# Weight sums and token forms on VectorE, and feed-forward buffers that stay open to the end of the block

## The chip, the cores and the metric

The kernel runs on one core of one Trainium2 chip. The metric is the device time of one execution in microseconds (us); the time of a kernel is the median of its runs. The engines of the core are TensorE (PE, matrix products; PEld is its weight load), VectorE (DVE), ScalarE (ACT), GpSimd (POOL) and SyncE (SP, which issues most of the transfers). Each works through its own instruction queue in order, and they wait for each other through semaphores.

## The reference: one encoder layer

One layer is applied to 768 tokens (512 of a prompt, 256 of a sample) of width 1024, all in float32:

```
x = LN1(alpha*x + 0.5*SwiGLU1(x))          # SwiGLU: (silu(x @ Wg) * (x @ Wu)) @ Wd, inner width 2816
u = x @ W_in                                # 5888 columns: RWKV-7 group, retention group, two gates
a = RWKV7_bidir(u_a) @ W_A ; b = Retention_bidir(u_b) @ W_B
x = LN2(alpha*x + (sigmoid(g_a)*a + sigmoid(g_b)*b) @ W_out)
x = LN3(alpha*x + 0.5*SwiGLU2(x))
```

The change touches the two feed-forward blocks (FFN1 with LN1, FFN2 with LN3), what follows FFN1 (the first two column blocks of W_in), and the buffers of the merge before LN2.

## The kernel before

**Layout.** Activations lie transposed: 8 tiles `z[k]` of 128 features by 768 tokens. A float32 product is made of three products of a rounded high part and a low part (high x high, high x low, low x high). `split` (lines 186 to 188) makes the parts: ScalarE casts the high part, VectorE subtracts it. `mmt` (line 198) issues all these products.

**The up projection** (`ffn`, from line 290) works on 22 blocks of 128 inner features, index j. A block needs two weights (gate g and up u, 512 KB each, "raw" loads at line 310 into 3 buffers `wr`) and two token halves of 384 (TH). Instead of eight half products it makes seven, in Strassen's manner: "11", "21", "22", "T1", "T2", "T3", "T4". Each is 12 matmuls of 384 columns. For that, it needs sums of weights and of tokens:

- weight sums s1 to s4, one set for each block, in `combine` (line 329) on GpSimd, 128x512 each. `pieces` splits each product's weight into high and low (tiles `ph`, `pl`, 4 buffers each).
- token forms t1 to t4, once for each FFN and each of four feature pairs, in `forms` (lines 276 to 288): t1 and t3 on GpSimd, t2 and t4 on VectorE, and then split into the second half of `xs[k]` (for T1) and into `ext` (tiles `eh`, `el`: T3, T4, T2).

`head(j)` (line 332) makes product 11, `second(j, g)` (line 341) adds 21 and applies silu, `do_up(j)` (line 346) makes the rest; additions at line 360 take the products out of PSUM. The first 2 blocks of FFN1 and the first 4 of FFN2 have head and second ahead of everything (`lead`), then load their gate weight again in FFN2.

**The down projection.** The blocks go in chunks of 6, 6, 5 and 5. `do_down` adds a chunk's product into `z` for all 768 tokens; it stands behind the first block of the next chunk. `last_down` (line 392) does the last chunk by token segments (512, then 256 tokens), so that LayerNorm of one segment can run beside the product of the other. Its weights come through `wtile` (lines 157 to 159): one load, a cast, a subtraction, into a pool `wp` of 2 buffers that is opened when the up projection's pools (`fw`: raw weights, pieces, sums; `xe`: `ext`) are closed (lines 416 and 417). 4 of the 8 weights of segment 0, and the last two of the rotating ones, are reused for segment 1 (`reuse`, line 174).

**LayerNorm** (`layer_norm`, line 250): the mean over features is a product with a matrix of 1/1024 on TensorE. `token_sum` (line 236) either does this for each of 8 feature tiles (8 matmuls that accumulate, line 239), or adds the tiles on VectorE (line 246) and makes one matmul (line 248). Tables MPE (mean) and VPE (variance) choose for each LayerNorm and segment; 1 means TensorE. Then come subtraction of the mean (line 259), squares on ScalarE (line 261), the variance, an inverse root by Ln and Exp (lines 230 to 234), scaling (lines 267 and 268) and, where something follows, a split.

**What follows FFN1.** `prep` begins with two lead products of W_in, blocks 12 and 13, weights through `wp`. Their place in TensorE's queue is fixed by hand (`issue_after`): the first behind the mean of segment 1, the second behind its variance, so that they run while LayerNorm of segment 1 is made. `prep` and the retention then load all further weights through `wp`.

**The merge** before LN2 loads W_out for three segments of 256 tokens, and KEEPO of its 8 weights are kept for the later ones.

**PSUM** has 8 banks of 512 columns. In FFN1 there are two tiles of two banks ("mm", one of them in a pool `pre`) for the down products and 4 single banks ("pc") for the up products and sums. In FFN2 the same with its own pool.

**Order.** A planner orders each engine's instructions at build time, by their order in the program and by when its model holds them to be ready; inside `prep` and the FFNs nothing but the leads is pinned by hand. A pool that is opened where another was closed waits for that pool's users.

Of the kernel before, what the change touches and what calls it, by code (L numbers as in the profile page):

```python
# [17 lines left out]
P = 128  # L18
# [31 lines left out]
MPE = {1: (0, 0), 2: (0, 0, 0), 3: (0, 0)}  # L50
VPE = {1: (0, 0), 2: (0, 0, 1), 3: (0, 1)}
# [4 lines left out]
KEEPO = 2  # L56
# [9 lines left out]
class Builder:  # L66
# [169 lines left out]
    def token_sum(self, st, src, k, pe, pool):  # L236
        nc = self.nc
        if pe:
            nc.tensor.matmul(st["ps"], self.ones, src, start=k == 0, stop=k == KT - 1)
            return  # L240
# [35 lines left out]
    def forms(self, z, xs, ext, tmp):  # L276
        nc = self.nc
        for k in range(KT // 2):
            (b11, b12), (b21, b22) = ([t[:, :TH], t[:, TH:]] for t in (z[k], z[k + KT // 2]))
            ta, tb = (tmp.tile([P, T], F32, tag=t, name=self.nm("f")) for t in ("hh", "hl"))  # L280
            t1, t2, t3, t4 = ta[:, :TH], ta[:, TH:], tb[:, :TH], tb[:, TH:]
            nc.gpsimd.tensor_tensor(out=t1, in0=b12, in1=b11, op=ALU.subtract)
            nc.gpsimd.tensor_tensor(out=t3, in0=b22, in1=b12, op=ALU.subtract)
            nc.vector.tensor_tensor(out=t2, in0=b22, in1=t1, op=ALU.subtract)
            nc.vector.tensor_tensor(out=t4, in0=b21, in1=t2, op=ALU.subtract)
            self.split(t1, *(t[:, TH:] for t in xs[k]))
            self.split(tb, *(t[:, :2 * TH] for t in ext[k]))
            self.split(t2, *(t[:, 2 * TH:] for t in ext[k]))

    def ffn(self, ctx, z, xs, idx, up, down, after, lead, first, wctx, then=None):  # L290
# [5 lines left out]
        hp = self.pool(ctx, "hp", max(CHUNKS) + 3, "right")  # L296
        hs, kept, raws, open_ = {}, {}, {}, {}
# [29 lines left out]
        def combine(a, b, op):  # L327
            t = fw.tile([P, m * P], F32, tag="sa", name=self.nm("sa"), bufs=4)
            nc.gpsimd.tensor_tensor(out=t, in0=a, in1=b, op=op)  # L329
            return t  # L330

        def head(j):
            g = load(j, 0)
            s, uu = (hp.tile([P, T], F32, tag=t, name=self.nm("u")) for t in ("hh", "hl"))
            ps = self.bank()[:, :TH]
            product(ps, g[:, :m * P], "11", True)
            nc.scalar.copy(uu[:, :TH], ps)
            open_[j] = s, uu, ps
            return g

        def second(j, g):
            s, uu, ps = open_[j]
# [3 lines left out]
        def do_up(j):  # L346
# [3 lines left out]
            s, uu, _ = open_[j]  # L350
# [5 lines left out]
            pc, pd, pb = (self.bank()[:, :TH] for _ in range(3))  # L356
# [35 lines left out]
        def last_down(seg, lp, kp):  # L392
# [3 lines left out]
            fetch = lambda n, keep=None: self.wtile(down[n, :, ch[0]:ch[-1] + 1], (len(ch), P), keep)  # L396
            for i, (n, w) in enumerate(self.reuse(kept, fetch, kp, KEEP)):
# [4 lines left out]
            return mean  # L402
# [142 lines left out]
    def prep(self, fill):  # L545
# [7 lines left out]
        if True:  # L553
# [5 lines left out]
            lead = [self.mmps() for _ in range(2)]  # L559
            lw = [self.wtile(self.I["w_in"][i], (KT, P)) for i in (12, 13)]  # L560
            var = self.summed
            with self.tc.issue_after(self.mean):
                self.mm3b(lead[0], lw[0], self.xs, SEGS[:1], len(BLK[1]) > 2)
            self.tc.add_manual_dep(var, self.latest.name, mybir.DependencyInfo(
                mybir.DependencyClass.NoSync, mybir.DependencyReason.DATA), reason="order")
# [618 lines left out]
```

## Time and profile before

| what | us |
|---|---|
| median of 3 runs | 1987.51 (1984.5 to 1987.61) |
| the profiled execution | 1985.87 |
| its span | 1984.1 |
| TensorE busy | 1870.1 |
| VectorE busy | 1240.4 |
| ScalarE busy | 833.2 |
| GpSimd busy | 486.5 |

Times in the profile count from the span's start. A line such as L198 is the line of the kernel's text that issued an instruction; since helpers issue most of them, the tile names on both sides tell more: `pc<-xh,ph` is a product into a single bank from activations `xh` and weight pieces `ph`. FFN1's up projection runs to 491 us, LN1 and the lead products to about 581 us, the merge and LN2 to about 1434 us, FFN2's up projection to 1911 us.

### The profile page before, as it was taken

Reading aid. Unit: us, or ns where it says so; the run is one execution under the profiler, and the core shown is the slowest. Engines: PE = TensorE matmul, PEld = TensorE weight load, DVE = VectorE, ACT = ScalarE, POOL = GpSimd, SP = SyncE. Lnnn points to the kernel's source line nnn. Section 1 sums busy time; section 2 is a strip of 40 time slices with the busy share of each in tenths; the row PEclk is TensorE's granted clock in tenths of the full one; section 3 lists DMA queues with packets and bytes.
Section 4 is the critical chain, followed back from the end, with each engine's and each line's share of the span. In section 5 each row is a group of like instructions: output and inputs, shape, how many; then the busy total and the mean of one; then the engine's idle time right before and its main releaser. Section 6 shows DMA issues by size and latency. Waiting matters only on the chain.

```text
span 1984.1 us, 33432 instructions
## 1 busy us (share of the span) xinstructions
PE 1870.1 (94%) x13224; PEld 1681.4 (85%) x13224; DVE 1240.4 (63%) x2064; ACT 833.2 (42%) x1512; POOL 486.5 (25%) x482
## 2 busy tenths in 40 slices
PE   6999999999979999999999988999779999999996
PEld 6999999999758777887888777789679999899985
DVE  8753745646675786768445556487777456365567
ACT  4432423424364453445355645334644234243334
POOL 5412303222000264445510000000164033131310
PEclk8999999999989999999999989999889999999998
DMA  4221221221242433333464442554222212212122
GB/s 133 75 67 62 76 74 64 61 78 46 79 143 86 148 117 127 109 129 116 142 207 127 128 114 90 196 194 146 75 76 72 78 64 71 69 64 74 65 68 73
DMA packets 115100, 197.48 MB, mean 100 GB/s; under 512 B 52736, under 2 KB 61312, under 8 KB 114944
## 3 DMA queue, kind: packets, MB, share of 16 engines
q1 hardware_dynamic: 97408, 173.32, 27.5%
q0 software_dynamic: 3424, 14.94, 2.3%
q10 hardware_dynamic: 14112, 7.08, 1.3%
q8 instruction: 105, 1.72, 0.4%
q14 instruction: 51, 0.42, 0.1%
HBM read 153.62 MB, written 41.68 MB: 98 GB/s over the span
## 4 chain that ended last, share of the span: by engine, by line
PE 81%; DVE 8%; ACT 4%; DMA 3%; issue 2%; POOL 1%; ACTq 0%; SPq 0%; DVEq 0%; POOLq 0%
PE mm L198 39%; PE pc L198 30%; PE pc L102 2%; PE mm L464 2%; ACT z L268 1%; PE pc L891 1%; POOL sa L329 1%; PE w L827 1%; PE w L838 1%; PE pc L939 1%; DMA wr<-in_f2u 1%; DVE z L259 1%; PE w L832 1%; PE pc L521 1%; DMA t<-gd 1%
## 5 line engine op out<-in xcount | busy, mean ns | idle before, releaser
L198 PE MATMUL pc<-xh,ph 128*128 128x384 f32 x704 | 241.4, 343 | 30.4 <-ACT xh L187 12.9
L187 ACT CAST ph<-wr 128x512 fp32r<-128x512 f32 (+1 forms) x228 | 129.1, 568 | 300.5 <-PE mm L198 180.2
L188 DVE TENSOR_TENSOR pl<-wr,ph 128x512 fp32r<-128x512 f32 (+1 forms) x228 | 174.7, 768 | 125.3 <-ACT ph L187 109.6
L198 PE MATMUL pc<-xl,ph 128*128 128x384 f32 x704 | 240.1, 341 | 0.2 <-DVE xl L188 0.2
L329 POOL TENSOR_TENSOR sa<-wr 128x512 f32<-128x512 f32 x44 | 70.1, 1593 | 626.5 <-DMA wr<-in_f1u 290.2
L360 DVE TENSOR_TENSOR u<-u,pc 128x384 f32<-128x384 f32 x220 | 121.0, 550 | 161.5 <-PE pc L198 160.0
L198 PE MATMUL mm<-xh,wh 128*128 128x512 f32 (+1 forms) x672 | 188.2, 356 | 18.1 <-ACT xh L187 8.5
L187 ACT CAST ph<-sa 128x512 fp32r<-128x512 f32 x176 | 109.2, 621 | 222.5 <-PE pc L198 160.0
L198 PE MATMUL mm<-xl,wh 128*128 128x512 f32 (+1 forms) x672 | 180.5, 346 | 2.6 <-DVE xl L188 2.6
L198 PE MATMUL pc<-eh,ph 128*128 128x384 f32 x528 | 178.0, 338 | 4.4 <-DVE u L360 4.1
L198 PE MATMUL pc<-el,ph 128*128 128x384 f32 x528 | 177.5, 336 | 0.2 <-DVE el L188 0.2
L188 DVE TENSOR_TENSOR pl<-sa,ph 128x512 fp32r<-128x512 f32 x176 | 143.3, 816 | 48.6 <-ACT ph L187 28.0
L198 PEld LDWEIGHTS pc<-xh,ph 128*128 128x128 f32 x704 | 135.9, 193 | 33.7 <-ACT xh L187 13.6
L158 ACT CAST wh<-wr 128x1024 fp32r<-128x1024 f32 (+2 forms) x96 | 85.7, 892 | 179.7 <-PE mm L198 133.0
L159 DVE TENSOR_TENSOR wl<-wr,wh 128x1024 fp32r<-128x1024 f32 (+2 forms) x96 | 100.9, 1051 | 93.4 <-PE mm L198 41.3
L198 PE MATMUL pc<-xh,pl 128*128 128x384 f32 x704 | 152.3, 338 | 3.1 <-DVE pl L188 3.1
L198 PEld LDWEIGHTS mm<-xh,wh 128*128 128x128 f32 x672 | 107.4, 192 | 42.6 <-ACT xh L187 9.7
L198 PE MATMUL mm<-hh,ph 128*128 128x512 f32 (+1 forms) x544 | 138.9, 336 | 0.0
L198 PE MATMUL mm<-hl,ph 128*128 128x512 f32 (+1 forms) x544 | 138.8, 336 | 0.0
L198 PEld LDWEIGHTS pc<-xl,ph 128*128 128x128 f32 x704 | 135.9, 193 | 0.6 <-DVE xl L188 0.6
L198 PE MATMUL mm<-xh,wl 128*128 128x512 f32 (+1 forms) x672 | 134.1, 348 | 0.0
L198 PEld LDWEIGHTS pc<-xh,pl 128*128 128x128 f32 x704 | 126.2, 190 | 3.7 <-DVE pl L188 3.7
(290 smaller groups left out, 4108.3 us busy)
## 6 DMA issues: line engine op xcount, KB each, us to landing
wr<-in_f2u SPq DMA_DIRECT2D x48, 512.0 KB, 3.5
wr<-in_f1u SPq DMA_DIRECT2D x44, 512.0 KB, 3.4
wr<-in_w_in SPq DMA_DIRECT2D x32, 512.0 KB, 3.5
wr<-in_w_out SPq DMA_DIRECT2D x16, 512.0 KB, 3.6
wr<-in_w_in SPq DMA_DIRECT2D x28, 256.0 KB, 3.4
wr<-in_f1d SPq DMA_DIRECT2D x16, 384.0 KB, 3.2
dd<-ar SPq DMA_DIRECT2D x8, 768.0 KB, 3.3
dd<-kb SPq DMA_DIRECT2D x8, 768.0 KB, 3.9
```

The source lines that it names most:

```text
L102: self.nc.tensor.matmul(ps, w, x[:, a:b], start=True, stop=True)
L158: nc.scalar.copy(hi, raw)
L159: nc.vector.tensor_tensor(out=lo, in0=raw, in1=hi.bitcast(F32), op=ALU.subtract)
L187: self.nc.scalar.copy(hi, src)
L188: self.nc.vector.tensor_tensor(out=lo, in0=src, in1=hi.bitcast(F32), op=ALU.subtract)
L198: self.latest = self.nc.tensor.matmul(o, w, x[:, a:b], start=start and i == 0, stop=stop and i == len(terms) - 1, skip_group_check=more).ins
L259: nc.vector.tensor_tensor(out=z[k][:, a:b], in0=z[k][:, a:b], in1=mean, op=ALU.subtract)
L268: nc.scalar.activation(zk, zk, AF.Identity, bias=self.vcol(g0 + 8 + k), scale=self.vcol(g0 + k))
L329: nc.gpsimd.tensor_tensor(out=t, in0=a, in1=b, op=op)
L360: add = lambda o, a, b: nc.vector.tensor_tensor(out=o, in0=a, in1=b, op=ALU.add)
L464: nc.tensor.matmul(dst, x[:, ts], w[:, :, k % 4], start=(k == 0 and q == 0), stop=(k == KT - 1 and q == 2))
L521: nc.tensor.matmul(op, v[:, a // P + j], x[:, j, :n], start=(j == 0 and q == 0), stop=(j == nj - 1 and q == 2))
```

## The change

1. **Engines.** All four weight sums and all four token forms run on VectorE. The forms are made product by product (t1 of all four pairs, then t3, t2, t4), each split on its own.
2. **Sums over features.** Segment 1's mean of LN1 and LN3 is made on TensorE, and so are the variances of both segments of LN1 and LN3.
3. **PSUM.** Three tiles of two banks ("mm") and 2 single banks ("pc") in both FFNs. The up products take a two-bank tile by pairs (`pairps`: 11 with T2, T1 with T3); a block of the lead takes a single bank for T2. The same PSUM pool goes on into `prep`, and from the merge into FFN2.
4. **Buffers.** `xe` and `fw` stay open to the end of the block. The last down projection loads its weights into the `wr` buffers of `fw` and splits them into `hp` (the pool of the block products, now 8 buffers for 9); the last 3 weights of a segment are held for the next, for 6 before. The lead weights of W_in go into `wr` and `xe`, and the lead products stand in `first`, still inside the block. `wp` is opened after the block. LayerNorm's pool has 3 buffers for 4.
5. **Merge.** KEEPO is 1 for 2, and the pool of kept weights lies below the others on the left side.

```diff
-MPE = {1: (0, 0), 2: (0, 0, 0), 3: (0, 0)}
-VPE = {1: (0, 0), 2: (0, 0, 1), 3: (0, 1)}
+MPE = {1: (0, 1), 2: (0, 0, 0), 3: (0, 1)}
+VPE = {1: (1, 1), 2: (0, 0, 1), 3: (1, 1)}
-KEEPO = 2
+KEEPO = 1
...
+    def pairps(self):
+        self.turn += 1
+        p = self.pre if self.pre and self.turn % (self.pb["mm"] + 1) == 0 else self.ps
+        t = p.tile([P, 2, 512], F32, tag="mm", name=self.nm("mm"), bufs=1 if p is self.pre else self.pb["mm"])
+        return t[:, 0, :TH], t[:, 1, :TH]
...
     def forms(self, z, xs, ext, tmp):
-            nc.gpsimd.tensor_tensor(out=t1, in0=b12, in1=b11, op=ALU.subtract)
-            nc.gpsimd.tensor_tensor(out=t3, in0=b22, in1=b12, op=ALU.subtract)
-            nc.vector.tensor_tensor(out=t2, in0=b22, in1=t1, op=ALU.subtract)
-            nc.vector.tensor_tensor(out=t4, in0=b21, in1=t2, op=ALU.subtract)
...
+        for k, (b11, b12, b21, b22) in enumerate(B):
+            sub(ta[k][:, :TH], b12, b11)
+            self.split(ta[k][:, :TH], *(t[:, TH:] for t in xs[k]))
+        tb = [tmp.tile([P, T], F32, tag="hl", name=self.nm("f")) for k in range(m)]
+        for k, (b11, b12, b21, b22) in enumerate(B):
+            sub(tb[k][:, :TH], b22, b12)
+            self.split(tb[k][:, :TH], *(t[:, :TH] for t in ext[k]))
...
-        hp = self.pool(ctx, "hp", max(CHUNKS) + 3, "right")
+        hp = self.pool(ctx, "hp", max(CHUNKS) + 2, "right")
-        cu = ctx.enter_context(ExitStack())
-        fw, xe = self.pool(cu, "fw", 1), self.pool(cu, "xe", 1)
+        xe, fw = self.pool(ctx, "xe", 1), self.pool(ctx, "fw", 1)
+        lp = self.pool(ctx, "lp", 3)
...
-            nc.gpsimd.tensor_tensor(out=t, in0=a, in1=b, op=op)
+            nc.vector.tensor_tensor(out=t, in0=a, in1=b, op=op)
...
+        def last_weights(n):
+            w = len(chunks[-1]) * P
+            r = raw(down[n, :, chunks[-1][0]:chunks[-1][-1] + 1])
+            h, l = (hp.tile([P, T], F32R, tag=t, name=self.nm("w"))[:, :w] for t in ("hh", "hl"))
+            self.split(r, h, l)
+            return tuple(t.rearrange("p (a b) -> p a b", b=P) for t in (h, l))
...
-        cu.close()
-        self.weights(wctx, D)
-        lp, kp = self.pool(ctx, "lp", 4), self.pool(ctx, "kp", KEEP)
+        held = {}
         for seg in BLK[idx]:
-            after(seg, last_down(seg, lp, kp), lp)
+            mean, held = last_down(seg, held)
+            after(seg, mean, lp)
+
+        def lead_weights(i, src):
+            r = raw(src)
+            h, l = (xe.tile([P, D], F32R, tag=f"{t}{i}", name=self.nm("w")) for t in ("eh", "el"))
+            self.split(r, h, l)
...
+            kp = self.pool(ctx, "kp", KEEPO)
             tq = self.pool(ctx, "tq", TQ)
             mp = self.pool(ctx, "mp", 8, "right")
-            kp = self.pool(ctx, "kp", KEEPO, "right")
...
-                self.psum(cw, pre, mm=1, pc=4)
+                self.psum(cw, pre, mm=2, pc=2)
                 with ExitStack() as ctx:
-                    self.first(ctx, cm)
-            with ExitStack() as cw:
-                self.psum(cw, pre, mm=2, pc=2)
+                    self.first(ctx)
+                self.weights(cm, D)
...
+            self.psum(cx, mm=3, pc=2)
             with ExitStack() as ctx:
-                self.psum(ctx, mm=3, pc=2)
...
-            self.psum(cx, mm=2, pc=4)
...
+        lead = self.lead = [self.mmps() for _ in range(2)]
+        lw = [weights(i, I["w_in"][12 + i]) for i in range(2)]
+        var = self.summed
+        with self.tc.issue_after(self.mean):
+            self.mm3(lead[0], lw[0], self.xs, SEGS[:1])
```

More of the change, by code (lines that the diff above doesn't have):

```diff
@@ L238, in token_sum @@
         if pe:
-            nc.tensor.matmul(st["ps"], self.ones, src, start=k == 0, stop=k == KT - 1)
+            self.summed = nc.tensor.matmul(st["ps"], self.ones, src, start=k == 0, stop=k == KT - 1).ins
             return
@@ L355, in do_up @@
             s4 = combine(q2[0], s2, ALU.subtract)
-            pc, pd, pb = (self.bank()[:, :TH] for _ in range(3))
+            pc, pd = self.pairps()
+            if early:
+                pb = self.bank()[:, :TH]
             product(pc, s1, "T1", True)
@@ L395, in last_down @@
             mean = {"ps": self.bank()[:, :b - a]}
-            fetch = lambda n, keep=None: self.wtile(down[n, :, ch[0]:ch[-1] + 1], (len(ch), P), keep)
-            for i, (n, w) in enumerate(self.reuse(kept, fetch, kp, KEEP)):
+            order = [n for n in held] + [n for n in range(KT) if n not in held]
+            now = dict(held)
+            for i, n in enumerate(order):
+                w = now[n] if n in held else last_weights(n)
+                now[n] = w
                 ps = self.mmps()
@@ L401, in last_down @@
                 self.token_sum(mean, z[n][:, a:b], i, MPE[idx][BLK[idx].index(seg)], lp)
-            return mean
+            return mean, {n: now[n] for n in order[KT - (max(CHUNKS) + 2 - len(ch)):]}
         first(load, ext, hp)
@@ L558, in prep @@
             lt = pp.tile([P, T], F32, name="lt")
[L559 to L565, printed above, removed]
-            with self.tc.issue_after(var):
-                self.mm3b(lead[1], lw[1], self.xs, SEGS[:1], len(BLK[1]) > 2)
-            for ps, w in zip(lead, lw):
-                self.mm3(ps, w, self.xs, SEGS[1:])
-            u = self.shift(12, self.t3("t"), lead[0])
+            u = self.shift(12, self.t3("t"), self.lead[0])
             nc.scalar.activation(lt[0:64], u[0:64], AF.Tanh)
             nc.scalar.copy(lt[64:P], u[64:P])
-            sg = self.shift(13, self.t3("r"), lead[1])
+            sg = self.shift(13, self.t3("r"), self.lead[1])
             nc.scalar.activation(sg, sg, AF.Tanh, scale=0.5)
@@ L1086, in build, with first @@
                 self.dump("x2", z[k], lambda d: d[:, k])
-            self.psum(cx, mm=2, pc=4)
             self.ffn(cx, z, self.xs, 3, I["f2u"], I["f2d"],
                      lambda seg, mean, lp: self.layer_norm(lp, z, 3, None, seg, mean, O["y"]),
-                     LEAD2, lambda load, ext, tmp: self.forms(z, self.xs, ext, tmp), cx)
-    def first(self, ctx, wctx):
+                     LEAD2, lambda load, ext, tmp: self.forms(z, self.xs, ext, tmp))
+    def first(self, ctx):
         nc, I = self.nc, self.I
@@ L1112, in after @@
             self.layer_norm(lp, z, 1, self.xs, seg, mean, self.x1d)
-        self.ffn(ctx, z, xs, 1, I["f1u"], I["f1d"], after, 2, inputs, wctx, self.consts)
+        weights = self.ffn(ctx, z, xs, 1, I["f1u"], I["f1d"], after, 2, inputs, self.consts)
+        lead = self.lead = [self.mmps() for _ in range(2)]
[3 more added lines that the diff above has]
+            self.mm3(lead[0], lw[0], self.xs, SEGS[:1])
+        self.tc.add_manual_dep(var, self.latest.name, mybir.DependencyInfo(
+            mybir.DependencyClass.NoSync, mybir.DependencyReason.DATA), reason="order")
+        with self.tc.issue_after(var):
+            self.mm3(lead[1], lw[1], self.xs, SEGS[:1])
+        for ps, w in zip(lead, lw):
+            self.mm3(ps, w, self.xs, SEGS[1:])
         for k in range(KT):
```

33 lines of the change are left out of this document (19 added, 14 removed).

## The prediction

> **What bounds the kernel now.** I read the busy times first, then stretches of the span, then TensorE's waits inside the stretches that are not full.
>
> ```profile
> span 1984.1 us, 33432 instructions
> PE 1870.1 (94%) x13224; PEld 1681.4 (85%) x13224; DVE 1240.4 (63%) x2064; ACT 833.2 (42%) x1512; POOL 486.5 (25%) x482
> ```
>
> TensorE bounds it: 114 us of the span are not TensorE's. Where they lie (columns: length, busy time of PE, PEld, DVE, ACT, POOL with instruction counts, granted clock, DMA share, GB/s):
>
> ```profile
> 30.00:40.00 10.00, 8.04 (x31) 7.73 (x32) 10.00 (x19) 5.81 (x11) 3.44 (x2) 0.66 0.05 21
> 40.00:50.00 10.00, 9.72 (x55) 9.19 (x54) 6.72 (x10) 3.55 (x6) 6.24 (x4) 1.00 0.36 112
> 50.00:62.00 12.00, 10.75 (x61) 10.35 (x60) 9.54 (x14) 4.54 (x8) 6.06 (x4) 1.00 0.18 61
> 200.00:300.00 100.00, 100.00 (x579) 96.38 (x578) 59.28 (x85) 36.52 (x64) 24.37 (x16) 1.00 0.24 74
> 300.00:400.00 100.00, 100.00 (x578) 96.87 (x577) 57.75 (x84) 36.83 (x64) 30.10 (x20) 1.00 0.21 68
> 546.00:553.00 7.00, 0.10 (x1) 0.00 (x0) 7.00 (x17) 3.66 (x8) 0.00 (x0) 0.72 0.32 109
> 1437.00:1450.00 13.00, 9.03 (x49) 8.23 (x48) 13.00 (x20) 10.23 (x19) 7.34 (x6) 1.00 0.12 41
> 1450.00:1456.00 6.00, 0.19 (x1) 0.19 (x2) 4.19 (x7) 0.62 (x1) 6.00 (x2) 0.51 0.00 0
> 1456.00:1467.00 11.00, 10.55 (x49) 10.23 (x49) 6.50 (x6) 4.36 (x8) 5.68 (x5) 0.80 0.30 98
> 1467.00:1479.00 12.00, 11.17 (x61) 10.35 (x62) 8.91 (x12) 4.16 (x7) 8.55 (x6) 1.00 0.36 118
> ```
>
> The middle of an FFN is full at full clock: 100/579 = 0.173 us a matmul there, and a faster VectorE or GpSimd buys nothing. The losses are at four ends: start of FFN1, its LayerNorm, start of FFN2, the tail. What ends TensorE's waits, for 480 to 620 us (first three) and 1390 to 1520 us (us in total, times, longest):
>
> ```profile
> PE mm L198 <- ACT xh L187: 8.5, 3, 7.1
> PE mm L198 <- issue: 3.9, 1, 3.9
> PE mm L198 <- DVE z L400: 2.0, 1, 2.0
> ...
> PE pc L198 <- ACT ph L187: 6.3, 2, 5.8
> PE pc L198 <- ACT xh L187: 5.8, 1, 5.8
> ```
>
> **GpSimd work moved to VectorE (token forms, weight sums).** 128x384 subtractions on VectorE before GpSimd's first (3.83/8 = 0.48 us each) and beside GpSimd's; GpSimd's own; and the first weight sum of FFN2 with the cast that waits for it (start, length, engine, line):
>
> ```profile
> 7.31 3.83 DVE L188 TENSOR_TENSOR xl<-z,xh 128x384 fp32r<-128x384 f32 x8
> 11.53 5.10 POOL L282 TENSOR_TENSOR f<-z 128x384 f32<-128x384 f32 x4 [11.07 <-DMA z<-in_xT]
> 15.70 1.34 DVE L284 TENSOR_TENSOR f<-z,f 128x384 f32<-128x384 f32 x1
> 1448.25 6.86 POOL L329 TENSOR_TENSOR sa<-wr 128x512 f32<-128x512 f32 x1 [5.66 <-issue]
> 1455.14 0.62 ACT L187 CAST ph<-sa 128x512 fp32r<-128x512 f32 x1 [5.56 <-POOL sa L329]
> ```
>
> The two engines delay each other: 1.34 us against 0.48 on VectorE, and a weight sum took 6.86 us while TensorE waited 5.8 for the cast behind it. In the steady part:
>
> ```profile
> L188 DVE TENSOR_TENSOR pl<-wr,ph 128x512 fp32r<-128x512 f32 x39 | 33.4, 855 | 19.1 <-ACT ph L187 17.1 <-PE pc L198 2.0
> L188 DVE TENSOR_TENSOR pl<-sa,ph 128x512 fp32r<-128x512 f32 x37 | 30.0, 811 | 7.9 <-ACT ph L187 5.2 <-PE mm L198 2.7
> L188 DVE TENSOR_TENSOR pl<-sa,ph x176: 677/686/1776, 35.1 to 1901.2; 128x512 fp32r<-128x512 f32 x176
> ```
>
> From 200 to 400 us VectorE is busy 117 us. The 36 sums that GpSimd ran there (its counts, 16 + 20) become 36 x 0.686 = +24.7 on VectorE; the splits fall to the median, 39 x 0.169 + 37 x 0.125 = -11.2. That gives 131 us of 200; without any relief, at 0.855 a sum, 148. VectorE stays off the bound, so the middle costs 0.
>
> The Trainium skill, SBUF — State Buffer, Who interferes with whom, says that a VectorE instruction with two SBUF inputs and a GpSimd instruction reading SBUF exclude each other, the later one blocking fully. The rows of the steady part show less, 0.13 to 0.17 us a split. By the rule, up to GpSimd's whole busy time there (24.4 + 30.1 us) would come back to VectorE, which would end near 87 of 200 instead of 131; the saturated VectorE of the slower rival would be less likely still.
>
> *Start of FFN1.* The forms are 32 instructions (16 subtractions, 16 splits) in VectorE's queue, 32 x 0.48 = 15 us from 11.5 on, when the last tokens are there. With four splits of tokens (1.9), two of pieces (1.4) and the first sum, its cast and split (2.0) ahead of T1, it comes at about 32 us, as now, if the queue runs all forms first, and at 11.5 + 3.8 + 5.3 = 21 if only T1's eight are ahead. After that, 31 + 55 + 61 = 147 matmuls now take 32 us and need 147 x 0.173 = 25.4: 6.6 are to be had, less some 2 for a clock that is still at 0.66 when it begins. Bounds -2 and -9; I take **-5**, near the first, since forms stand ahead of the sums in program order.
>
> *Start of FFN2.* 49 + 1 + 49 + 61 matmuls from 1437 to 1479 need 27.7 us and take 42, so 14 are lost, and the 5.8 before them (xh) shrink by perhaps 4, because the new pool order lets the first weights land before w_out's pool is free, out of LayerNorm's way. The forms still need 15 us of VectorE from about 1432, so T1 comes between 1440 and 1449 for 1455.8; behind it no sum waits for GpSimd, and the 0.80 clock of the next 11 us (2.2) goes with the pause. Bounds -6 (late T1, the 5.8 kept) and -18 (all of it); I take **-11**.
>
> **Pools kept open.** Now the last down projection's first weight waits for the closing pool:
>
> ```profile
> 491.19 6.58 SPq L157 DMA_DIRECT2D wr<-in_f1d  x4
> 494.23 0.72 ACT L158 CAST wh<-wr 128x640 fp32r<-128x640 f32 x1 [1.95 <-DMA wr<-in_f1d]
> 495.05 0.77 PE L198 MATMUL mm<-hh,wh 128*128 128x512 f32 x1 [3.92 <-issue]
> 495.00:500.00 5.00, 4.95 (x16) 3.98 (x17) 2.42 (x3) 1.31 (x2) 0.00 (x0) 0.72 0.47 131
> 534.00:546.00 12.00, 10.28 (x64) 9.16 (x64) 11.51 (x24) 7.12 (x9) 0.00 (x0) 0.86 0.12 32
> ```
>
> The last up product ends at 491.1. With its raw weights in a pool already open that 3.9 goes, with 5 x 0.28 = 1.4 of slow clock behind it; late next are the last block's own parts hh and hl (I estimate 1.6 of waiting, from two additions, a product, a cast and a split of 0.5 to 1 us each, less the two microseconds that TensorE has with the other blocks). **-3.7** in each FFN. Three shared PSUM tiles instead of two let segment 1 run on while VectorE subtracts segment 0's mean: the 2.0 pause goes, and 12 x 0.14 = 1.7 of slow clock after it: -3.7 again.
>
> The Trainium skill, TensorE: The Clock Gate, What's actually happening, has the clock fall after an idle window of about 3.4 us. Here a pause of 2.0 us was followed by 12 us at 0.86, so by the row that pause costs 3.7; by the rule it would cost 2.0, and the segment's gain would be 1.7 smaller.
>
> What the pools move is the wait itself. The projections' pool (wp) now opens only when FFN1's pools close, after the two lead products. Its first load then has nothing ahead of it but the last lead matmul. Its price, from the landing time of 512 KB and one cast of 1024 columns:
>
> ```profile
> wr<-in_w_in SPq DMA_DIRECT2D x32, 512.0 KB, 3.5
> 579.43 1.05 ACT L158 CAST wh<-wr 128x1024 fp32r<-128x1024 f32 x1 [2.04 <-PE mm L198]
> ```
>
> 3.5 + 1.05 = 4.6, and 1.4 of slow clock as behind the 3.9: **+6** (0 if addresses rather than whole pools decide, since the lead weights lie in one part of `xe`). Queued behind that load on SP are the next weights, `lora` and the retention's tables; who waits for those, the shift and the rope, stands behind TensorE's next products anyway.
>
> **Sums on TensorE.** One 512-column sum costs TensorE 0.87 us, one of 256 costs 0.45; then VectorE's additions, ScalarE's work at the end of the tail, VectorE's eight subtractions of segment 0's mean, and the stretch of the merge that takes the added loads:
>
> ```profile
> 543.25 0.87 PE pc L248 x2
> 567.56 0.45 PE pc L248 x2
> L246 DVE TENSOR_TENSOR acc<-acc,ln 128x512 f32<-128x512 f32 (+1 forms) x12 | 6.6, 549 | 0.4 <-ACT ln L261 0.3
> 1973.03 8.25 ACT L268 ACTIVATE z<-z,vec 128x512 f32<-128x512 f32 x14
> ...
> 529.26 4.78 DVE z L259 x8
> 1390.00:1410.00 20.00, 20.00 (x171) 19.95 (x170) 16.35 (x38) 10.16 (x20) 0.00 (x0) 1.00 0.16 53
> ```
>
> Segment 0's variance: 7 x 0.87 = +6.1 on TensorE; segment 1's mean: 7 x 0.45 = +3.1; its variance the same (already there in FFN2). VectorE loses seven additions for each, 7 x 0.55 = 3.8 us. In FFN1 the mean of segment 1 (546.1, where the 7 us stretch begins) comes at 546.1 - 3.7 - 3.7 + 9.2 = 547.9. But segment 0's variance, now at 544.1, can end 2 us behind the eight subtractions (534.0), 8 to 12 us sooner with the earlier start, so its activations exist when the lead products want them, and most of the 8.5 on xh goes. The leads need 48 matmuls of 512 and 48 of 256 columns, by columns from 0.173 us: 48 x 0.231 + 48 x 0.115 = 16.6; the variance's sums 3.6, waits 2: they end at 570, now at 581.4. **-11 + 6 = -5**; bounds -11 (no pool wait) and +4 (activations as late as now). In the tail the same +1.8 on the mean stands against ScalarE's 14 activations in 8.25 us: segment 0's are done before, and some 4 us fall away. **-2**; bounds -5 and +3.
>
> KEEPO 1 adds two w_out loads, two casts of 1.05 and two splits, hidden behind a TensorE that is full to 1410 with VectorE at 16.4 of 20: 0, bound +2. Fewer held down weights (3 for 6) add three loads in segment 1 of each FFN, of 0.72 us on ScalarE and about as much on VectorE; the sums on TensorE cover them: 0. Without that cover +2 in each, which the upper bounds hold.
>
> Sum: -5 - 5 - 11 - 2 = -23 on the profiled 1985.9 us (span 1984.1 and 1.8 around it). The runs' median is 1987.5, so **1964** for the median.
>
> **Rivals.** *More of it*: the planner puts T1's forms and the sums ahead, and addresses decide the pool: -9 - 10 - 15 - 4 = -38, 1949. For it: the forms' loops are now split by product. Against it: forms precede sums in the program.
> *Only FFN2 gains*: the sums on TensorE and the moved pool wait eat LayerNorm and tail (+2, +2), start -3, FFN2 -8: 1980.
> *No change*: raw weights' DMAs, not GpSimd, end the waits at both starts, and the losses cancel the rest. In its favour, the chain of waits holds such a load beside the sums:
>
> ```profile
> 1460.16 4.66 DMA wr<-in_f2u
> ```
>
> Against it: the load could only start when GpSimd's sums and the splits had freed its buffer, and they come sooner.
> *Slower*: sums in VectorE's queue wait for a late raw load and hold the evacuations and splits behind them. The place is the 44 up blocks; the early blocks already pause TensorE for one late addition:
>
> ```profile
> 50.15 0.56 DVE u L360
> ```
>
> If each block paused so, it would cost 44 x 0.56 = 25 and cancel the 23; from 0.52 us a block it decides, and at 1 us, +44 - 23 = +21: 2008. Against it: VectorE at two thirds, four piece buffers ahead of TensorE.
>
> **Numbers.** Forecast 0.50 (1955 to 1973), more 0.15, only FFN2 0.17, no change 0.07, slower 0.11. Faster by over 0.2% (4 us, about what can be told here) 0.82, same 0.07, slower 0.11. The range, from 1946 to 1986, leaves out half of "more", the slower case and a little of the rest.
>
> **What would show it.** Right: no GpSimd work in the FFNs, splits near 0.69 us throughout; no 3.9 pause ahead of the last down projection; T1 of FFN2 near 1445 minus the earlier gains; a pause of about 4.6 behind the lead products, ended by a load of in_w_in. Wrong: TensorE below 99% in the middle of an FFN, waits on VectorE's splits there; xh still late after segment 1's mean; a tail ended by TensorE's sums.

## The result, and the profile after

The changed kernel takes **2252.6 us** (median; 2250.7 to 2255.4), beside 1987.6 us for the kernel before on the same chip: a ratio of 1.133, 95% interval 1.129 to 1.136. It is 265 us slower; the forecast was 1964 us, with a range from 1946 to 1986.

First the page's busy times, the longest waits of TensorE over the whole span (us in total, times, longest), and the two stretches in the middle of FFN1 that were full before (length, busy time of PE, PEld, DVE, ACT, POOL with counts, granted clock, DMA share, GB/s):

```profile
span 2253.4 us, 33277 instructions
PE 1958.2 (87%) x13294; PEld 1751.0 (78%) x13294; DVE 1274.6 (57%) x2237; ACT 844.1 (37%) x1528; POOL 191.2 (8%) x290
...
PE mm L204 <- ACT u L349: 180.3, 34, 7.7
...
PE mm L204 <- ACT w L193: 6.4, 2, 3.2
...
200.00:300.00 100.00, 82.78 (x436) 79.58 (x435) 52.10 (x82) 28.79 (x49) 0.00 (x0) 0.90 0.14 49
300.00:400.00 100.00, 90.22 (x494) 83.59 (x492) 43.78 (x68) 24.65 (x44) 0.00 (x0) 0.95 0.19 58
```

GpSimd has left the feed-forward blocks, as planned. But the middle is no longer full: 436 and 494 matmuls in 100 us for 579 and 578. One wait dominates, 34 times in the 38 up blocks behind the early ones: a matmul waits for ScalarE's copy in line 349, the evacuation of product 11 (its way out of PSUM). VectorE is not saturated; it is *less* busy than before (52.1 and 43.8 of 100).

Where the time went, by landmarks. These are the lines' own views (duration min/median/max, first and last start), first before, then after: subtraction of LN1's mean (its first start), the shift behind the lead products, retention's first values, the scan (last start), the up blocks' first SiLU (last start):

```profile
L259 DVE TENSOR_TENSOR z<-z,pc x56: 409/414/682, 529.2 to 1967.0; 128x256 f32<-128x256 f32 x40, 128x512 f32<-128x512 f32 x16
L571 ACT ACTIVATE lt<-t x1: 847/847/847, 587.0 to 587.0; 64x768 f32<-64x768 f32 x1
L470 ACT COPY v<-mm x4: 799/799/801, 604.1 to 802.0; 128x768 f32<-128x768 f32 x4
L816 PE MATMUL w<-S,ar x320: 216/218/267, 1026.6 to 1262.6; 64*64 64x64 f32 x160
L344 ACT ACTIVATE u<-pc x44: 484/493/494, 30.7 to 1906.6; 128x384 f32<-128x384 f32 x44
```

```profile
L265 DVE TENSOR_TENSOR z<-z,pc x56: 406/412/689, 657.2 to 2238.3; 128x256 f32<-128x256 f32 x40, 128x512 f32<-128x512 f32 x16
L591 ACT ACTIVATE lt<-t x1: 842/842/842, 720.4 to 720.4; 64x768 f32<-64x768 f32 x1
L501 ACT COPY v<-mm x4: 799/800/801, 744.2 to 941.8; 128x768 f32<-128x768 f32 x4
L836 PE MATMUL w<-S,ar x320: 216/218/267, 1166.1 to 1406.2; 64*64 64x64 f32 x160
L356 ACT ACTIVATE u<-mm x44: 490/493/500, 20.5 to 2169.6; 128x384 f32<-128x384 f32 x44
```

| stretch | before | after | difference |
|---|---|---|---|
| start to LN1's mean subtracted | 529.2 | 657.2 | +128.0 |
| to the first shift (LN1, lead products) | 57.8 | 63.2 | +5.4 |
| to retention's first values (the moved pool wait) | 17.1 | 23.8 | +6.7 |
| to the scan's last of these products | 658.5 | 662.0 | +3.5 |
| to the last up block's SiLU (merge, FFN2) | 644.0 | 763.4 | +119.4 |
| to the end (tail) | 77.5 | 83.8 | +6.3 |

They sum to 269.3, the difference of the spans. Nearly all of it lies in the two stretches that hold the feed-forward blocks (the second holds the merge too).

One later up block shows how. All engines of the after kernel around 305 us (start, length, engine, line; in brackets the idle time before and what ended it):

```profile
301.12 0.33 SPq L322 DMA_DIRECT2D wr<-in_f1u  x1
...
303.44 1.03 PE L204 MATMUL mm<-eh,pl 128*128 128x384 f32 x5
303.64 0.62 ACT L193 CAST ph<-wr 128x512 fp32r<-128x512 f32 x1 [1.23 <-PE mm L204]
...
304.63 0.69 DVE L341 TENSOR_TENSOR sa<-wr 128x512 f32<-128x512 f32 x1 [3.53 <-DMA wr<-in_f1u]
...
305.84 0.55 DVE L374 TENSOR_TENSOR u<-u,mm 128x384 f32<-128x384 f32 x1
306.31 0.68 DVE L194 TENSOR_TENSOR pl<-sa,ph 128x512 fp32r<-128x512 f32 x1
306.91 0.68 DVE L194 TENSOR_TENSOR pl<-wr,ph 128x512 fp32r<-128x512 f32 x1
...
308.11 0.95 DVE L385 TENSOR_TENSOR u<-u,u 128x768 f32<-128x768 f32 x1
...
309.15 0.83 ACT L193 CAST hh<-u 128x768 fp32r<-128x768 f32 x1 [4.89 <-DVE u L385]
309.89 0.47 ACT L349 COPY u<-mm 128x384 f32<-128x384 f32 x1
...
310.41 0.69 PE L204 MATMUL mm<-eh,ph 128*128 128x384 f32 x1 [5.94 <-ACT u L349]
```

Read it backwards. At 310.41 product T2 of the next block starts; it waited 5.94 us for the copy of product 11 at 309.89. That copy's matmuls were long done, but ScalarE's queue holds the present block's cast `hh` (309.15) ahead of it, and this cast waits for VectorE's multiplication (308.11), the last step of the block. VectorE comes late to it because it stood 3.53 us at its first weight sum (304.63), whose raw load went out only at 301.12. So two queues each wait at an entry that is not what TensorE needs.

Why T2 needs the copy at all: `pairps` gives product 11 and T2 two halves of one two-bank tile. T2's own inputs were there earlier: ScalarE's last cast of a weight piece ahead of it ended at 304.26 (303.64 + 0.62), VectorE's last split of one at 307.59 (306.91 + 0.68). T2 started 0.05 us after the copy's end (309.89 + 0.47), and the profile names this copy as the releaser 34 times. Before the change each product had a tile of its own, and this tie did not exist. The halves are different banks (the second begins 512 floats on), so the wait comes from the tile, not from the bank; the experiments below test it. The Trainium skill, Perfetto Trace Analysis, Matmuls, advises to rotate independent matmul groups through different PSUM banks, so that the evacuation of one overlaps the next group; here the banks differ and the overlap is lost all the same.

Behind the wait TensorE is slow for a while (windows as above):

```profile
310.00:313.00 3.00, 2.59 (x8) 2.59 (x9) 0.96 (x1) 0.36 (x1) 0.00 (x0) 0.50 0.05 17
313.00:316.00 3.00, 3.00 (x11) 3.00 (x10) 1.27 (x3) 0.62 (x1) 0.00 (x0) 0.50 0.00 0
316.00:320.00 4.00, 4.00 (x24) 4.00 (x24) 1.93 (x4) 1.74 (x3) 0.00 (x0) 0.98 0.00 0
```

From 310.4 to about 316 it runs at half clock, which costs 2.8 us more. If all 34 waits were followed so, that is 180 of waiting and up to 95 of clock: enough for the 128.0 and 119.4. The mean granted clock points the same way: 0.934 over 2253.4 us is 149 us below full clock, 0.971 over 1984.1 us was 58 (idle time included).

### The profile page after: what moved, and what is told of

It is laid out like the page before. It is cut to its first block, busy times and chain, and to the rows that moved or that the text cites. A ratio compares the mean times of both kernels' runs of the same rounds, so it can differ in the third digit from the quotient of the medians.

```text
span 2253.4 us, 33277 instructions
## 1 busy us (share of the span) xinstructions
PE 1958.2 (87%) x13294; PEld 1751.0 (78%) x13294; DVE 1274.6 (57%) x2237; ACT 844.1 (37%) x1528; POOL 191.2 (8%) x290
## 4 chain that ended last, share of the span: by engine, by line
PE 70%; DVE 14%; DMA 7%; issue 4%; ACT 4%; ACTq 0%; SPq 0%; DVEq 0%; POOLq 0%
PE mm L204 59%; DVE pl L194 3%; DMA wr<-in_f1u 2%; DVE sa L341 2%; DMA wr<-in_f2u 2%; PE pc L108 2%; PE mm L495 2%; DVE u L385 1%; PE pc L245 1%; DMA t<-gd 1%; PE pc L911 1%; DVE u L374 1%; ACT z L274 1%; ACT u L349 1%; DVE f L285 1%
## 5 line engine op out<-in xcount | busy, mean ns | idle before, releaser
L204 PE MATMUL mm<-eh,ph 128*128 128x384 f32 x504 | 193.9, 385 | 174.8 <-ACT u L349 172.4
L204 PE MATMUL mm<-xh,ph 128*128 128x384 f32 x704 | 248.8, 354 | 28.9 <-ACT ph L193 10.4
L204 PE MATMUL mm<-xl,ph 128*128 128x384 f32 x704 | 244.4, 348 | 0.2 <-DVE xl L194 0.2
L374 DVE TENSOR_TENSOR u<-u,mm 128x384 f32<-128x384 f32 x214 | 117.7, 551 | 216.4 <-PE mm L204 214.7
L204 PE MATMUL mm<-el,ph 128*128 128x384 f32 x504 | 189.2, 375 | 0.0
L204 PEld LDWEIGHTS mm<-xh,ph 128*128 128x128 f32 x704 | 141.5, 201 | 36.7 <-ACT ph L193 14.9
L204 PE MATMUL mm<-xh,pl 128*128 128x384 f32 x704 | 148.4, 339 | 0.1
L204 PEld LDWEIGHTS mm<-xl,ph 128*128 128x128 f32 x704 | 140.4, 200 | 0.8 <-DVE xl L194 0.6
L204 PEld LDWEIGHTS mm<-xh,pl 128*128 128x128 f32 x704 | 126.5, 191 | 1.0 <-DVE pl L194 1.0
L204 PE MATMUL mm<-eh,pl 128*128 128x384 f32 x504 | 124.8, 375 | 0.0
```

Of the source, the lines that this page charges most:

```text
L204: self.latest = self.nc.tensor.matmul(o, w, x[:, a:b], start=start and i == 0, stop=stop and i == len(terms) - 1, skip_group_check=more).ins
L374: add = lambda o, a, b: nc.vector.tensor_tensor(out=o, in0=a, in1=b, op=ALU.add)
```

## The experiments

Two theories stood at first: VectorE's queue stands at late loads (the queue), or T2 is tied to product 11 (the tile). All ratios are to the kernel before, run beside them; its median lay between 1989.6 and 1992.8 us.

**Taken from the changed kernel, one cause at a time.**

Sums back on GpSimd:

```
-            nc.vector.tensor_tensor(out=t, in0=a, in1=b, op=op)
+            nc.gpsimd.tensor_tensor(out=t, in0=a, in1=b, op=op)
```

> The changed kernel with the four weight sums back on GpSimd; all else as changed. Queue theory (VectorE stands at a block's first sum until the up weight has landed, 3.4 to 3.5 us a block, and everything behind it in its queue is late): the wait goes back to an engine with nothing behind it, TensorE's waits on the copy of product 11 (180 us) all but vanish, 1950 to 1990 us. Shared-tile theory (it is T2's place in the tile of product 11 that costs, since T2 then waits for that copy, which stands behind a block's cast): the copy is still behind the cast, half a microsecond to one a block with its clock stays, 2010 to 2060 us.

Measured 2276.1 us, ratio 1.142 (1.138 to 1.146), above both bands. VectorE no longer stands at the load, and T2's wait stays, as the waits and ScalarE's and VectorE's rows of such a block show:

```profile
PE mm L204 <- ACT u L349: 194.2, 34, 7.0
...
312.33 1.74 DVE L194 TENSOR_TENSOR pl<-sa,ph 128x512 fp32r<-128x512 f32 x1
313.99 1.75 DVE L194 TENSOR_TENSOR pl<-wr,ph 128x512 fp32r<-128x512 f32 x1
315.66 2.01 DVE L385 TENSOR_TENSOR u<-u,u 128x768 f32<-128x768 f32 x1
...
317.76 0.83 ACT L193 CAST hh<-u 128x768 fp32r<-128x768 f32 x1 [5.97 <-DVE u L385]
318.50 0.47 ACT L349 COPY u<-mm 128x384 f32<-128x384 f32 x1
```

Now VectorE reaches its multiplication late because each step beside GpSimd's sum takes 1.7 to 2.0 us instead of 0.7 to 0.95. The queue theory by itself falls: whatever delays the multiplication delays T2.

T2 in a bank of its own, in every block and not only in the early ones:

```
-            if early:
-                pb = self.bank()[:, :TH]
+            pb = self.bank()[:, :TH]
```

> The changed kernel, but T2 gets a single bank of its own in every block, not only in the lead blocks; sums stay on VectorE. Shared-tile theory: the loss goes, 2000 us or less. Queue theory: VectorE stands still as before; T2 (12 matmuls, 2.1 us) covers that much of each wait in some 34 blocks, with less half clock: 2130 to 2190 us, VectorE's waits for raw loads still above 3 us each.

Measured 2085.0 us, ratio 1.047 (1.044 to 1.050): 168 us come back. Waits on the copy fall to 22.3 us. More than the queue theory allowed, less than the tile theory asked.

Four raw buffers, so that the load no longer waits for the split just ahead:

```
-            t = fw.tile([P, D], F32, tag="wr", name=self.nm("wr"), bufs=3)
+            t = fw.tile([P, D], F32, tag="wr", name=self.nm("wr"), bufs=4)
```

(room for it: `lp` has 2 buffers instead of 3, and one accumulator instead of 2)

> The changed kernel with four raw weight buffers for three, so that the up weight's load need not wait for the split just ahead of the sum; to make room LayerNorm's pool in the FFNs has 2 buffers for 3 and one accumulator for two. Sums and shared tile stay. Queue theory: VectorE no longer stands at the sums, TensorE full in the blocks, 1955 to 2000 us (LayerNorm up to 10 us slower is in that). Shared-tile theory and a theory that VectorE is simply too full with the sums: 2150 us or more.

Measured 2187.4 us, ratio 1.099 (1.095 to 1.102): 65 us come back, within the band of the tile theory. The wait of T2 shrinks to 129.2 us in the same 34 places; it does not go.

And the sums on VectorE alone, in the kernel before (the edit above the other way round):

> The kernel before with only the four weight sums on VectorE; T2 has its own bank there, forms on GpSimd. Queue theory: VectorE waits for the loads here too, T2 covers part: 2050 to 2150 us. Shared-tile theory: 2010 us or less.

Measured 2024.8 us, ratio 1.017 (1.014 to 1.019), between the two bands. The sums alone cost 34 us, 0.8 us for each of 44 blocks. What TensorE waits for then, and the middle of FFN1:

```profile
PE pc L198 <- DVE u L360: 21.0, 32, 1.3
PE pc L198 <- ACT u L337: 13.8, 13, 6.1
...
200.00:300.00 100.00, 95.68 (x541) 90.89 (x540) 62.59 (x100) 36.19 (x63) 0.00 (x0) 1.00 0.21 65
300.00:400.00 100.00, 96.81 (x550) 91.45 (x549) 59.40 (x94) 33.93 (x58) 0.00 (x0) 1.00 0.18 64
```

These are the late additions of the prediction's slower rival. Both causes exist, then, and VectorE's standing feeds T2's wait: with the load in time (four buffers, above) that wait was shorter.

**The copy's place.** Is it the tie that is dear, or that the copy stands behind the cast? Tiles and engines as changed, but the next block's product 11 and copy are written ahead of the block's last split (not in a chunk's first block):

```
-            early = j in open_
-            g = load(j, 0) if early else head(j)
+            early = j < lead
+            g = load(j, 0) if j in open_ else head(j)
...
+            if j + 1 < chunks[-1][-1] + 1 and j + 1 not in open_ and j not in [c[0] for c in chunks[1:]]:
+                head(j + 1)
             hs[j] = tuple(hp.tile([P, T], F32R, tag=t, name=self.nm(t)) for t in ("hh", "hl"))
             self.split(s, *hs[j])
```

> The changed kernel, two-bank tiles and sums on VectorE as they are, but the next block's product 11 and its copy are written in the program ahead of the last split of the block, in all blocks but the first of each chunk, so that ScalarE's queue holds the copy ahead of the cast hh that waits for VectorE's multiplication. Theory, the shared tile costs its 168 us because T2 waits for a copy that stands behind that cast: most of it comes back, 2080 to 2130 us, TensorE's waits on the copy fall from 180 us to under 60. Rival, tying T2 to product 11 costs by itself, wherever the copy stands (or the wait moves to another link of the tile): over 2200 us.

Measured 2047.9 us, ratio 1.029 (1.027 to 1.031): **205 us come back** with the shared tile kept, more than the theory expected. The copy now stands ahead of the cast `hh` (in one block at 341.05, the cast at 353.69), and in the middle of FFN1 TensorE's products alternate as in the changed kernel, three on `ext` and four on `xs`. Its longest waits of TensorE, and the middle of FFN1:

```profile
PE mm L204 <- DVE u L374: 26.6, 29, 1.4
...
200.00:300.00 100.00, 96.06 (x540) 90.45 (x540) 60.39 (x98) 35.89 (x62) 0.00 (x0) 1.00 0.21 66
300.00:400.00 100.00, 96.60 (x547) 90.87 (x546) 56.51 (x91) 33.54 (x58) 0.00 (x0) 1.00 0.18 63
```

The wait on the copy is gone from the longest (7.0 us in 2 places are left); late additions of at most 1.4 us remain, and the clock stays at 1.00. The other cause, VectorE's standing at raw loads, is still there; in the changed kernel and then here its waits are 105.8 and 81.6 us:

```profile
DVE sa L341 <- DMA wr<-in_f1u: 56.6, 19, 5.3
DVE sa L341 <- DMA wr<-in_f2u: 49.2, 17, 3.9
...
DVE sa L341 <- DMA wr<-in_f1u: 43.6, 19, 3.4
DVE sa L341 <- DMA wr<-in_f2u: 38.0, 19, 4.1
```

The main cause is settled: a tie that costs little becomes dear through what stands ahead of the copy in ScalarE's queue.

**The tiles of before.** Every product in one of four single banks again, in FFN1 and FFN2 (and `psum(mm=1, pc=4)`, `psum(mm=2, pc=4)` around them), the rest as changed:

```
-            ps, pb = self.pairps()
+            ps = self.bank()[:, :TH]
...
-            pc, pd = self.pairps()
-            if early:
-                pb = self.bank()[:, :TH]
+            pc, pd, pb = (self.bank()[:, :TH] for _ in range(3))
```

This with the sums on VectorE; with four raw buffers besides; and instead with the sums on GpSimd:

> The changed kernel with only the PSUM tiles of the kernel before; weight sums on VectorE as changed. Theory, tiles are the larger cause: of the 265 us this takes back about 230, to 2010 to 2035 us, as with the sums alone moved in the kernel before (2025). Rival, T2's shared tile was all that was wrong with the tiles: as with T2 in a bank of its own, 2075 to 2095 us.

> As before, PSUM tiles of the kernel before and weight sums on VectorE, and four buffers for raw weights instead of three, with one scratch tile and one accumulator of LayerNorm less. If VectorE's standing at the up weight's load is what the sums on VectorE cost, this ends within 1 per cent of the kernel before, 1975 to 2005 us, with TensorE over 98% busy between 200 and 400 us. Rival, the sums on VectorE delay its additions even so: 2015 to 2035 us.

> The changed kernel with the PSUM tiles of the kernel before (each product of an up block in a bank of its own out of four, no two-bank tiles in FFN1, FFN2 and its merge) and the weight sums on GpSimd again; token forms on VectorE, open pools, later projection weights, and sums of LayerNorm on TensorE stay changed. Theory, the two-bank tiles are the larger cause (they tie products to each other and change the order in which TensorE takes them) and the sums on VectorE the smaller: this falls to the kernel before less the forms' 8.5 us and the first down weights' 2 x 3.7, plus 7 for LayerNorm's sums and 8 for the pool wait: 1991 us, within 1975 to 2000. Rival, the open pools or their order hold a cost in the up blocks that no run has shown: over 2030 us.

Measured 2047.4 (ratio 1.028, 1.026 to 1.030), 2010.3 (1.010, 1.008 to 1.012) and 2015.0 us (1.012, 1.009 to 1.014). So the old tiles give back 205 us with the sums on VectorE, as much as moving the copy did, and 261 with the sums on GpSimd (from 2276.1); a load in time gives another 37. All three lie 5 to 15 us above the bands expected: the ends cost more than I had summed. With four buffers the middle of FFN1 is what it was before:

```profile
200.00:300.00 100.00, 100.00 (x578) 95.87 (x578) 61.12 (x99) 35.10 (x61) 0.00 (x0) 1.00 0.22 73
300.00:400.00 100.00, 100.00 (x579) 96.89 (x578) 63.08 (x101) 36.73 (x64) 0.00 (x0) 1.00 0.19 61
```

One reservation: with sums on VectorE and three buffers the planned order of products on TensorE differs from that of before (in the kernel before with the sums alone, too), and with four it is that of before again. The 37 us, and the 34 above, hold the standing at the load and that order together; no run told them apart.

T2's own bank with either remedy for the sums:

> The changed kernel with T2 in a bank of its own and with four buffers for raw weights instead of three (one scratch tile of LayerNorm and one of its two accumulators are given up for the fourth), so that an up weight's load no longer waits for the split just ahead of it; the sums stay on VectorE. If the sums on VectorE cost time only because VectorE stands at that load, the 98 us by which the kernel with T2's own bank is above the kernel before vanish for the most part: 1965 to 2000 us, with under 20 us of VectorE's waits on loads in the sums. Rival, VectorE as such is too slow or too late for its queue (splits and additions behind the sums): over 2040 us, with TensorE's waits on VectorE's splits where they were (24 us) or longer.

> The changed kernel with the product T2 in a bank of its own and the weight sums on GpSimd again: both causes found so far are taken away, and the rest of the change stays (token forms on VectorE, the pools that stay open, the later projection weights, the sums of LayerNorm on TensorE). If the shared tile and the sums on VectorE are all that was missed, and the prediction's other terms hold without the sums' part (start of FFN1 -5, start of FFN2 -6, first down weights 2 x -3.7, mean pause -3.7, LayerNorm -5, tail -2, and 3 for the pool wait of 7.9 instead of 4.6), it takes 1991 - 26 = 1965 us. Rival, the ends lose as much as they gain: 1985 to 2000 us. Rival, something else in the up blocks is still slower: over 2010 us, with TensorE below 97% between 200 and 400 us.

Measured 2062.9 us (ratio 1.036, 1.034 to 1.037), a miss, and 2144.0 us (1.075, 1.072 to 1.079), a large one. In the first, VectorE's waits for raw loads fell from 94.0 to 9.6 us and TensorE's on VectorE's splits (23.7 us) went, yet only 22 us came back: what is left are waits for evacuations (22.0 us on the copy, 13.1 on additions, 9.6 on SiLU). In the second, with GpSimd beside VectorE, TensorE waited 76.0 us for VectorE's splits. T1 and T3 are still paired in both; whether that is the cause of what is left was not tested.

**What is left at the ends.** With the old tiles and four buffers or GpSimd's sums, 20 to 24 us are left, and FFN1's middle is full. In the kernel with the old tiles and sums on GpSimd, TensorE waits at the merge's start for a load of `ybd`:

```profile
1229.56 1.01 SPq L1002 DMA_DIRECT2D t<-ybd  x2
1273.84 1.26 SPq L1002 DMA_DIRECT2D t<-ybd  x2
...
1285.14 1.65 PE L204 MATMUL mm<-yh,wh 128*128 128x512 f32 x3 [9.26 <-ACT yh L193]
```

In the kernel before, these loads went out while the scan still ran:

```profile
1224.17 1.05 SPq L984 DMA_DIRECT2D t<-ybd  x2
1231.77 1.95 SPq L984 DMA_DIRECT2D t<-ybd  x2
1237.38 1.87 SPq L984 DMA_DIRECT2D t<-gd  x2
```

The merge's pools as before (on the kernel with old tiles and four raw buffers):

```
-            kp = self.pool(ctx, "kp", KEEPO)
             tq = self.pool(ctx, "tq", TQ)
             mp = self.pool(ctx, "mp", 8, "right")
+            kp = self.pool(ctx, "kp", KEEPO, "right")
```

(and `KEEPO = 2`)

> The kernel with the PSUM tiles of before, sums on VectorE and four raw buffers (20 us above the kernel before, all at the ends), with the merge's pools as before the change: two held w_out tiles on the right side, behind mp, instead of one that opens first on the left. In the profile of its sister TensorE waits 9.3 us at the merge's start for a load of ybd that goes out only after the scan, with some 4 us of slow clock behind; in the kernel before there is no such wait. If the pool's place is the cause, this is 10 to 14 us faster than its pair: 1996 to 2000 us. Rival, the later pool of w_in or the order of the scan makes those loads late: no change, 2008 to 2012.

Measured 2004.0 us (ratio 1.006, 1.005 to 1.008), 6 us better than its pair, though the two intervals just overlap. In the two traces the stretch from the last start of the scan's products to the last of the additions that take FFN2's first down product into `z` falls from 338.9 to 329.5 us, the second pair of `ybd` loads goes out during the scan again, and the wait is gone. So the merge's pools are the cause; their place and their size (KEEPO) changed together. The gain in the median is smaller than the 10 to 14 expected.

LayerNorm's sums moved alone in the kernel before (with the line that marks the last sum for the leads), the reverse edit on the kernel with the old tiles and sums on GpSimd, and the forms alone in the kernel before:

```
-MPE = {1: (0, 0), 2: (0, 0, 0), 3: (0, 0)}
-VPE = {1: (0, 0), 2: (0, 0, 1), 3: (0, 1)}
+MPE = {1: (0, 1), 2: (0, 0, 0), 3: (0, 1)}
+VPE = {1: (1, 1), 2: (0, 0, 1), 3: (1, 1)}
```

> The kernel before with nothing but the sums over the 1024 columns in LayerNorm 1 and 3 moved to TensorE. By the prediction's terms: +6.1 and +3.1 of TensorE's work in LayerNorm 1 against up to 8.5 of the wait on xh, +1.8 against some 4 in the tail: 1991 - 2 = 1989 us, within 1984 to 1995 us. Rival, the activations come as late as before and the sums are paid in full: 1998 to 2005 us. Rival, the wait on xh goes and the freed VectorE brings more: under 1984 us.

Measured 1995.8 us (ratio 1.0033, 1.0016 to 1.0050): a loss of 6.6 us by the ratio and 3.0 by the medians (four of its ten runs lie above 2000 us, the others below 1997), between the first band and the first rival's.

> As the kernel with the PSUM tiles of before and the sums of weights on GpSimd, but the sums in LayerNorm 1 and 3 are VectorE's again, as before the change. Alone on the kernel before, moving them to TensorE cost 0.33%, 6.6 us; if that holds here, this is 5 to 8 us faster than its pair, and 0.2 to 0.8% faster than the kernel before (forms alone: 0.42%). Rival, with the pools open the freed VectorE brings something and the two are equal within 3 us.

Measured 2010.3 us (1.0098, 1.0079 to 1.0117) beside 2015.0 for its pair (1.0115, 1.0094 to 1.0137): the intervals overlap, not settled there.

> The kernel before with nothing but the token forms in the new order and on VectorE; weight sums stay on GpSimd. By the prediction's terms: start of FFN1 -5 (T1's tokens first), start of FFN2 some -6, since GpSimd has no forms ahead of its first weight sum: 1991 - 11 = 1980 us. Rival, the forms only move the wait to GpSimd's first sums and to VectorE's queue: 1987 to 1995 us. Rival, they lose: over 1995 us.

(The edit is the new `forms` of the diff, and nothing else.) Measured 1983.3 us (0.9958, 0.9942 to 0.9975), 8.4 us faster by the ratio: the forms are the change's good part. Its trace places only 1.5 us of this (below); the rest stays open.

All found causes mended at once, two-bank tiles kept (the edits above for the copy, the raw buffers and the merge):

> The changed kernel with three mends: the copy of product 11 written ahead of the block's last split, four raw buffers (LayerNorm gives up one scratch tile and one accumulator), and the merge's pools as before. Two-bank tiles, sums and forms on VectorE, open pools and sums of LayerNorm on TensorE stay. If the copy's place, the standing at the load and the merge's pool are the three things that made the change slow, their gains add: 2048 - 37 - 6 = 2005 us, within 1993 to 2012, TensorE over 98% busy between 200 and 400 us, and what is left lies at the ends. Rival, the two-bank tiles cost by themselves another 20 to 50 us: 2025 to 2050 us.

Measured 2010.2 us (1.0102, 1.0080 to 1.0123), inside the first theory's band. In its middle 566 and 567 matmuls run in 100 us for 579 and 578, with TensorE 99.93 busy by the page: with the paired tiles some 2% stay lost that show as no wait. Their order of products differs from that of before as well; no run told tile and order apart.

**A version that beats both.** The kernel before with the new forms, sums on VectorE and four raw buffers, which fit there because its pools close before the last down projection:

> The kernel before with three things only: token forms in the new order on VectorE, weight sums on VectorE, and four raw buffers instead of three, which fit because its pools close before the last down projection. If VectorE's standing at the load was all that the sums on VectorE cost, the forms' 8.5 us (0.42%) stay and FFN2's start gains from sums that come at 0.7 us instead of 6.9: 1970 to 1982 us. Rival, the sums still delay VectorE in the starts: 1985 to 1995 us.

Measured **1974.0 us**, ratio 0.991 (0.990 to 0.993): 17 us faster than before, in the band. Its middle is full, with VectorE at 61.7 and 63.4:

```profile
200.00:300.00 100.00, 100.00 (x579) 95.99 (x578) 61.69 (x99) 35.69 (x62) 0.00 (x0) 1.00 0.22 72
300.00:400.00 100.00, 100.00 (x579) 96.89 (x578) 63.43 (x101) 36.72 (x64) 0.00 (x0) 1.00 0.19 63
```

## Why the prediction was wrong, step by step

- **"VectorE stays off the bound, so the middle costs 0."** This step failed, and with it the forecast: the two stretches with the feed-forward blocks cost 128.0 and 119.4 us more. The busy sum itself was good: 131 of 200 was forecast, and where the middle is full again VectorE does 125.1 (61.7 + 63.4). What it left out is order. A VectorE at 60% still stands 3.5 us at one late load, with additions and splits behind it.
- **The two-bank tiles were costed only as a third PSUM tile for the last down projection** (-3.7; that pause did go). That the same lines tie T2 to product 11 in all the up blocks behind the early ones was in the diff, and no term was made for it. It is the larger cause: moving the copy, or restoring the tiles, gave back 205 us each. The question to ask was what stands ahead of the copy in ScalarE's queue: it is the cast `hh`.
- **The slower rival** named VectorE's queue at a late raw load with additions behind it, decided from 0.52 us a block. Alone it did just that, at 0.8 us a block (34 us over 44 blocks). Its argument against, "four piece buffers ahead of TensorE", did not hold: the buffer that counts is the raw one, and it is freed by the split just ahead. As price of the whole change 2008 was far short, because it had no tile in it.
- **Start of FFN1, -5.** The first SiLU comes at 20.5 for 30.7 us, but the gain at the first additions of the down projection is 1.5 us with the forms alone (136.4 for 137.9) and 2.2 to 4.4 with the old tiles and a full middle (133.5 to 135.7). Right in kind, too large.
- **Start of FFN2, -11.** With the merge's pools restored, from the scan's end to those additions in FFN2 329.5 for 338.2 us: -8.7, near the forecast. The gain comes with the sums, or with the buffer beside them, not with the forms or the open pools: with the forms alone the stretch takes 338.5, in the fastest kernel, which adds the sums and the fourth buffer and closes its pools as before, 330.0.
- **First down weights, -3.7 in each FFN.** The pause only changed its ender: two of 3.2 us (first fence) for two of 3.9. The slow clock behind it went (1.00 for 0.72 in FFN1), so about 2 of the 3.7 came. "Late next" was named rightly, the last block's own parts, and mis-sized (1.6): the new weights' casts also stand behind that block's cast `hh` in ScalarE's queue.
- **The moved pool wait, +6.** Measured +6.7 between the shift and the values; its row is a pause of 7.9 us instead of 4.6:

```profile
PE mm L204 <- ACT wh L164: 7.9, 1, 7.9
```

- **LayerNorm 1 without that wait, -11.** It is +5.4 in its stretch: the wait on `xh` shrank from 8.5 to 3.4 us, but the sums were paid and the wait on the low parts grew from 2.6 to 5.2. The sign was wrong; the step that failed is that most of the 8.5 would be profit. Alone in the kernel before, the sums took the wait on `xh` away and still did not shorten this stretch (59.0 for 57.8 us). In the new layout they do help it, 60.0 us against 66.3 with the sums on VectorE (old tiles, sums of weights on GpSimd); so a part of the loss comes from the layout, and which part of it was not tested.
- **Tail, -2 (with the 7.4 from weights and tile in it).** +6.3. TensorE's sums waited 6.7 us for ScalarE's squares there; "a tail ended by TensorE's sums" was on the list of what would prove it wrong. Moved alone in the kernel before they make it 4.7 longer (82.2 for 77.5 us); but with them back on VectorE and the old tiles it still takes 82.9, so the layout has a share that no run separates.
- **KEEPO 1, 0.** The edit also moved a pool to the left and ahead of the others, and the merge's second pair of loads goes out after the scan: 9.4 us in the traces. I costed the extra loads and not what the pools wait for.

## What to carry to other kernels

An engine's busy share says nothing about what stands at the head of its queue: when work moves to an in-order queue, or an output moves into a shared tile, name for each block the entry that will wait, what frees it, and who is behind it. Here a tile shared by two outputs made the writer of the second wait for the reader of the first, and that reader was only as prompt as the entry ahead of it; writing it earlier in the program may cure what looks like a matter of buffers. Before moving work to a faster engine, check that its inputs' buffers are not freed by the instruction just ahead of it in the same queue: here a fourth buffer and the new forms together turned a loss of 34 us into a gain of 17, of which the forms alone give 8.

## What the runs showed that I had not expected

Pauses above some microseconds are dearer than their length: after 5.94 us the clock was 0.50 for some 5.6 us more, while with the copy first 29 waits of up to 1.4 us left it at 1.00 in the middle of FFN1. The Trainium skill, TensorE: Matmul & The Clock Gate, What's actually happening, has the slow state follow an idle window of about 3.4 us; these two rows agree with it. Length alone does not decide, though: a pause of 3.2 us ahead of each last down projection was followed by the full clock, 1.00, and one of 2.0 us in the kernel before by 12 us at a mean of 0.86. And GpSimd's sum beside VectorE can hurt more than moving it helps (2276.1 us beside 2252.6): in the changed layout VectorE's 0.95 us multiplication took 2.01 beside it.
